# A trunk layer on one core: a bank of its own for the third product of a first pair, a norm stream that waits by GpSimd's price, and new prices for the planner

## The chip, the core and the metric

One core of one Trainium2 chip. The metric is the device time of the whole kernel in microseconds (us), the median of several runs. Engines are called by the profile's names: PE (TensorE), PEld (its weight loads), DVE (VectorE), ACT (ScalarE), POOL (GpSimd) and SP (SyncE, which issues the weight loads from memory).

## The reference

One layer of a streaming encoder, for 512 prompt tokens and 8x16 sample tokens (T = 640 in all), model width 1024, in fp32:

```python
z = x @ w_in
xa, ya, glu, q, gates = jnp.split(z, COL_SPLITS, axis=-1)
xa_c = causal_depthwise_conv(xa_hist, conv_a_w, conv_a_b)          # width 4
h, h_last = rg_lru(xa_c, h_prev, w_r, b_r, w_i, b_i, lam)          # gated linear scan
out_a = (h * jax.nn.gelu(ya)) @ proj_a
u = glu[..., :D_CONV] * jax.nn.sigmoid(glu[..., D_CONV:])
v = causal_depthwise_conv(u_hist, conv_b_w, conv_b_b)              # width 31
out_b = jax.nn.silu(layer_norm(v, ln_b_g, ln_b_b)) @ proj_b
out_c = mem_cross_attention(q, mem_k, mem_v) @ proj_c              # 4 heads, 256 memory tokens
merged = g[:, :, 0] * out_a + g[:, :, 1] * out_b + g[:, :, 2] * out_c
x = layer_norm(ALPHA * x + merged @ w_out, ln1_g, ln1_b)
ffn = (silu(x @ w_ffn_gate) * (x @ w_ffn_up)) @ w_ffn_down
x = layer_norm(ALPHA * x + ffn, ln2_g, ln2_b)
```

Prompt and sample tokens have different histories, states and memories: the prompt's memory is projected from mem_prompt, the sample's eight memories come from the caches cache_mem_k and cache_mem_v. The outputs are x, the new states and the prompt's memory.

## The kernel before

**Products.** Activations lie transposed, channels on the partitions and the 640 tokens along a row, in two halves of HT = 320 columns. Each fp32 product is made of three fp32r matmuls: the weight and the activation are each split in a high part (a rounded copy, written by ACT) and a low part (a subtract, on DVE, for some early weights on POOL, L305), and PE adds hi·hi, hi·lo and lo·hi in one PSUM bank. In the views `wh`/`wl` are the parts of a weight, `xh`/`xl` those of the layer's input, `s` is any tile of the common pool of row buffers, `pu` is a PSUM bank of the main loop (four buffers) and `pv` one of the side work (two buffers, counted in `side`).

**The main loop** runs over 304 steps, each with prep_hi (ACT), prep_lo, mm (PE) and an evacuation that is put off until the next flush. The order of the steps: mem_k and mem_v projections 0 to 7, the GLU and the query to 19, xa 20 to 27, the gates of branch C 28 to 35, proj_c 36 to 43 (from 304.3 us), the gates of branch B alternating with proj_b 44 to 59, ya 60 to 67, the gates of branch A 68 to 95, proj_a 96 to 103 (from 542.8 us), w_out to 116 (to 672 us), then the FFN, whose pairs begin with step 120 (686 us).

**Pairs.** The gates of branch A and the FFN's first two products take two 128-column blocks of weights at once and spend seven products in place of eight (`seven`): sums of weight blocks (on DVE) times sums of activation quarters (the streams sums0 and sums1, on DVE with a split by ACT and DVE). The first pair of each group uses the order m1, m4, m2, m6, m5, m7, m3. m1 goes to bank x; ACT copies it to `tmp["a"]`; the third product, m2, is then added in the same bank x, which so holds m1 + m2, one quarter of the result. m2's matmuls must therefore wait for the copy.

**Streams.** All other work is written as generators ("streams") that a planner interleaves with the main loop: attn (the cross-attention of prompt and sample), b (the width-31 conv and then ln_b_stream, its norm), lru (conv a, the gates r and i, the scan), a (times gelu, split in high and low for proj_a), the sums, the norms. The planner runs when the program is written, not on the chip, and it goes by prices: every instruction issued through `Engine` adds its price to that engine's time. After pieces of a step's matmuls `advance()` takes items of a stream as long as DVE's and ACT's priced times lie behind PE's:

```python
while max(V.time, 0 if name in vector_next else A.time) < P.time:
    c = next(gen)
    ...
    if c is None:
        break
```

A `yield None` in a stream thus means: no more of this stream in this call. `room()` holds a stream until a side bank is free, `over()` gives one back. `finish(name)` issues at once all that is left of a stream, ahead of the step that needs it: `finish("attn")` before proj_c (step 36), `finish("b")` before the first proj_b step (46), `finish("lru", "a")` before proj_a (96), the first sums before the pairs (the rows of the sums with the steps 68 and 120).

**The norm of branch B** (ln_b_stream). `total` adds the four rows of channels on POOL (L853 once, L855 twice); PE multiplies the sum with a matrix of ones to have it on all partitions; DVE subtracts, ACT squares; a second total; a second matmul; rs = pow on POOL (L892); then multiply, Silu and split, which gives bT for proj_b.

**The sample attention** (attn_sample). The keys and values of the caches are loaded by POOL's queue, one head of eight memories as four loads (L1069). After scores and softmax come the transposes of the probabilities, then for each head h 16 small matmuls (32 rows of output each) with the values of head h, which give back that head's four buffers. The tail copies the output, transposes it four times and splits it to cT for proj_c.

POOL itself isn't priced before the change; its queue runs in the order in which the planner issued it.

Of the kernel before, what the change touches and what calls it, by code (L numbers as in the profile page):

```python
# [11 lines left out]
OP = mybir.AluOpType  # L12
# [8 lines left out]
HT = T // 2  # L21
# [46 lines left out]
def elements(x):  # L68
    n = 1
    for d in x.shape[1:]:  # L70
        n *= d
    return n


def price_vector(e, name, a, k):
    if name in ("tensor_reduce", "bn_stats"):
        return 70 + elements(a[1]) / 0.96
    n = elements(a[0])
    if name == "tensor_tensor_scan":
        return 70 + 2 * n / 0.96  # L80
    if name in ("tensor_scalar", "tensor_copy", "memset"):
        return 70 + n / 1.92
    return (130 if name == "scalar_tensor_tensor" else 70) + n / 0.96


TABLES = {AF.Exp: "e", AF.Tanh: "esgl", AF.Sigmoid: "s", AF.Sqrt: "q", AF.Silu: "l", AF.Gelu_apprx_tanh: "g"}
# [2 lines left out]
def price_scalar(e, name, a, k):  # L89
    if name != "activation":  # L90
        return 100
    t = 130 + elements(a[0]) / 1.2
    t += 93 * sum(1 for z in ("scale", "bias", "accum_out") if z in k and not isinstance(k[z], float))
    need = TABLES.get(a[2])
    if need is not None and (e.table is None or e.table not in need):
        e.table = need[0]
        t += 1283
    return t


def price_tensor(e, name, a, k):
    n = elements(a[0])
    if a[1].dtype == F32R:
        return n / 2.4 + 2.5
    if a[0].shape[0] == 32:
        return n / 2.4
    return max(105.0, (n if name == "transpose" else 4 * n) / 2.4)
# [36 lines left out]
def trunk(ctx, tc, x_prompt, x_sample, mem_prompt, state_conv_a, state_lru, state_conv_b, cache_mem_k, cache_mem_v,  # L144
# [4 lines left out]
          new_conv_a_s, new_lru_s, new_conv_b_s):  # L149
    nc = tc.nc  # L150
    V, A, P = Engine(nc.vector, price_vector), Engine(nc.scalar, price_scalar), Engine(nc.tensor, price_tensor)
    G, S = nc.gpsimd, nc.sync

    w_in, proj_a, proj_b, proj_c, w_out = w_in[0], proj_a[0], proj_b[0], proj_c[0], w_out[0]
    w_mem_k, w_mem_v = w_mem_k[0], w_mem_v[0]
# [23 lines left out]
    def pv():  # L179
        assert side[0] < 2  # L180
        side[0] += 1
        return ps.tile([128, 2, 512], F32, name="pv", tag="v", bufs=2)

    def room(n=1):
        while side[0] + n > 2:
            yield None

    def over(n=1):
        side[0] -= n
# [134 lines left out]

    def advance(few=False):

        for e in (V, A):
            e.time = max(e.time, state["since"])
        state["since"] = P.time
        for item in list(streams):  # L330
            name, gen = item
            if few and name not in often:
                continue
            while max(V.time, 0 if name in vector_next else A.time) < P.time:
                try:
                    c = next(gen)
                except StopIteration:
                    streams.remove(item)
                    done.add(name)
                    break  # L340
                vector_next.discard(name)
                if c is None:
                    break
                if c == "v":
                    vector_next.add(name)

    def until(cond):

# [501 lines left out]
    def ln_b_stream():  # L850
        def total(x):
            y = get([128, T])
            G.tensor_tensor(y, x[0], x[1], op=OP.add)  # L853
            for k in range(2, KC):
                G.tensor_tensor(y, y, x[k], op=OP.add)  # L855
            return y

        y = total(vb)
        yield 1
        yield None  # L860
        yield from room()
        p = pv()
        P.matmul(p[:, 0], ones, y[:, :512], start=True, stop=True)
        P.matmul(p[:, 1, :128], ones, y[:, 512:], start=True, stop=True)
        free(y)
        yield None
        over()
        sq = []
        for k in range(KC):
            V.tensor_sub(vb[k][:, :512], vb[k][:, :512], p[:, 0])  # L870
            V.tensor_sub(vb[k][:, 512:], vb[k][:, 512:], p[:, 1, :128])
            x = get([128, T])
            A.activation(x, vb[k], AF.Square)
            sq.append(x)
            yield 1
        y = total(sq)
        free(*sq)
        yield 1
        yield None
        yield None  # L880
        yield from room()
        p = pv()

        for t in range(5):
            P.matmul(p[:, 0, t * 100:(t + 1) * 100], y[:, t * 128:(t + 1) * 128], ones[:, :100], start=True, stop=True)
        free(y)
        yield None
        over()
        ve = small.tile([128, 5], F32, name="ve5")
        V.tensor_scalar(ve, p[:, 0, :500].rearrange("p (t n) -> p t n", n=100)[:, :, 0], EPS, None, op0=OP.add)  # L890
        rs = small.tile([128, 5], F32, name="rs5")
        G.tensor_tensor(rs, ve, mhalf[:, :5], op=OP.pow)  # L892
        yield 1
        yield from room()
        p = token_row(rs)
        yield None
        over()
        for k in range(KC):
            V.tensor_mul(vb[k][:, :512], vb[k][:, :512], p[:, 0])
            V.tensor_mul(vb[k][:, 512:], vb[k][:, 512:], p[:, 1, :128])  # L900
            yield 1
        for k in range(KC):
            A.activation(vb[k], vb[k], AF.Silu, scale=pb[:, k, 32:33], bias=pb[:, k, 33:34])
# [603 lines left out]
    def seven(pair, put, following, first=False):  # L1507

        acc, tmp, late = {}, {}, []

        def fourth(p):
            put(0, 1, p, tmp["b"][:, 0], OP.subtract)

        def fifth(p):
            put(1, 1, p, tmp["b"][:, 0], OP.add)
            if first:
                V.tensor_tensor(tmp["a"][:, 1], tmp["a"][:, 1], p, op=OP.add)

        def after(n, p):
            if n == "m1":  # L1520
                tmp["a"], tmp["b"] = get([128, 2, HT]), get([128, 2, HT])
                copy(tmp["a"][:, 0], p)
            elif n == "m6":
                V.tensor_tensor(tmp["a"][:, 1], tmp["a"][:, 0], p, op=OP.add)
            elif n == "m2":
                put(0, 0, p, None, None)
            elif n == "m7":
                V.tensor_tensor(tmp["b"][:, 0], tmp["a"][:, 0], p, op=OP.add)
                for f in late:
                    f()  # L1530
            elif n in ("m4", "m5"):
                f = lambda: (fourth if n == "m4" else fifth)(p)
                if first:
                    late.append(f)
                else:
                    f()
            else:
                free(tmp["b"])
                put(1, 0, p, tmp["a"][:, 1], OP.add)
                free(tmp["a"])  # L1540

        products = PRODUCTS
        if first:

            products = [PRODUCTS[i] for i in (0, 5, 2, 1, 4, 3)] + [("m3", "x", True, "s4", "22")]
        for i, (n, u, opens, xn, wn) in enumerate(products):
            def mm(w, u=u, opens=opens, xn=xn):
                if opens:
                    acc[u] = pu(1)[0][:, :HT]
                p = acc[u]  # L1550
                hi, lo = w
                xhi, xlo = quarters[xn]
                for k in range(half):
                    P.matmul(p, hi[:, k], xhi[k], start=opens and k == 0, stop=False, skip_group_check=not opens)
# [404 lines left out]
```

## Time and profile before

| | us |
|---|---|
| median of 3 runs | 1100.15 |
| the runs | 1099.13, 1100.15, 1100.48 |
| the profiled run | 1099.67 |
| its span in the profile | 1097.9 |
| PE busy | 1061.7 (97%) |
| DVE busy | 802.9 (73%) |
| ACT busy | 490.1 (45%) |
| POOL busy | 165.3 (15%) |
| granted TensorE clock, mean | 0.99 |

The span runs from the first to the last instruction of the profile; the run's own time is 1.8 us longer. In the timeline a row has its start, its length, engine, line, operation and tiles; a number in brackets is the engine's idle time just before it, with what ended it. Nearly every instruction is issued in the helper at L64, so that a line says little: the tile names tell which step it is. POOL's instructions before the change are not issued through that helper and so keep their lines.

### The profile page before, as it was taken

How to read it: one execution, taken by the hardware profiler on the slowest of the kernel's cores; microseconds unless marked ns; L12 is line 12 of the kernel's file. 1: busy time of each engine (PE TensorE's matmuls, PEld its weight loads, DVE VectorE, ACT ScalarE, POOL GpSimd, SP SyncE). 2: the span in 40 equal slices, each digit the busy share in tenths (PEclk: the TensorE clock that was granted, in tenths of full speed). 3: DMA queues.
4: the chain of work that ended last, by engine and by line, in shares of the span. 5: the costliest groups of instructions: out<-in, count | busy, mean ns of one | idle time of the engine just before them, and what ended most of it. 6: DMA issues, size and time to landing. Idle time of an engine off the chain costs nothing.

```text
span 1097.9 us, 17000 instructions
## 1 busy us (share of the span) xinstructions
PE 1061.7 (97%) x6827; PEld 1005.9 (92%) x6827; DVE 802.9 (73%) x1335; ACT 490.1 (45%) x863; POOL 165.3 (15%) x185
## 2 busy tenths in 40 slices
PE   8799898998999999999999999899999999999997
PEld 6699898997999999999999889899999999888886
DVE  6929898996364873779855678888887887544775
ACT  4532645446648445846523124433444444334341
POOL 3623323556200000010001120000000000100111
PEclk9999999998999999999999999999999999999999
DMA  9732123352412121212325331132222322734481
GB/s 340 253 95 78 39 67 97 118 154 65 147 52 83 59 96 59 95 45 78 115 78 172 135 134 59 39 101 92 77 78 85 108 77 78 287 115 137 162 289 45
DMA packets 80334, 123.11 MB, mean 112 GB/s; under 512 B 4075, under 2 KB 59371, under 8 KB 80256
## 3 DMA queue, kind: packets, MB, share of 16 engines
q1 hardware_dynamic: 73168, 100.36, 27.6%
q0 software_dynamic: 7088, 21.68, 6.2%
q8 instruction: 53, 0.87, 0.3%
q14 instruction: 25, 0.20, 0.1%
HBM read 112.41 MB, written 9.61 MB: 111 GB/s over the span
## 4 chain that ended last, share of the span: by engine, by line
PE 70%; DVE 11%; ACT 4%; issue 1%; DVEq 0%; ACTq 0%
PE pu L64 62%; DVE s L64 10%; PE pv L64 8%; ACT s L64 3%; ACT L64 1%; DVE wl L64 1%; ACT wh L64 0%; DVE xres L64 0%; DVE mx L64 0%; DVE wh L64 0%; DVE xl L64 0%; DVE nm L64 0%; DVEq L1955 0%; ACT wl L64 0%; DVE st L64 0%
## 5 line engine op out<-in xcount | busy, mean ns | idle before, releaser
L64 PE MATMUL pu<-xh,wh 128*128 128x320 f32 x1040 | 252.6, 315 | 8.3 <-ACT s L64 7.1
L64 PE MATMUL pu<-xh,wl 128*128 128x320 f32 x1040 | 246.9, 310 | 0.0
L64 ACT ACTIVATE wh<-wr 128x1024 fp32r<-128x1024 f32 (+1 forms) x149 | 134.9, 908 | 229.1 <-PE pu L64 123.2
L64 PE MATMUL pu<-xl,wh 128*128 128x320 f32 x888 | 219.7, 311 | 0.0
L64 PEld LDWEIGHTS pu<-xh,wh 128*128 128x128 f32 x1040 | 178.1, 190 | 13.2 <-ACT s L64 9.1
L64 PE MATMUL pu<-s,wh 128*128 128x320 f32 x1064 | 185.5, 310 | 1.9 <-DVE s L64 1.3
L64 PEld LDWEIGHTS pu<-xh,wl 128*128 128x128 f32 x1040 | 177.4, 189 | 0.1
L64 DVE TENSOR_TENSOR s<-s,s 128x640 fp32r<-128x640 f32 (+4 forms) x176 | 124.5, 723 | 65.5 <-ACT s L64 63.3
L64 PEld LDWEIGHTS pu<-s,wh 128*128 128x128 f32 x1064 | 163.4, 188 | 3.4 <-DVE s L64 2.4
L64 DVE TENSOR_TENSOR wl<-wr,wh 128x1024 fp32r<-128x1024 f32 (+1 forms) x100 | 114.1, 1141 | 66.7 <-ACT wh L64 66.7
L64 PEld LDWEIGHTS pu<-xl,wh 128*128 128x128 f32 x888 | 154.2, 189 | 0.6 <-DVE xl L64 0.6
L64 DVE TENSOR_TENSOR s<-s,pu 128x320 f32<-128x320 f32 x188 | 88.4, 484 | 85.8 <-PE pu L64 83.3
L64 PE MATMUL pu<-s,wl 128*128 128x320 f32 x808 | 147.3, 310 | 0.9 <-DVE s L64 0.9
L64 DVE SCALAR_TENSOR_TENSOR s<-s,pb,s 128x511 f32<-128x511 f32 (+14 forms) x240 | 130.1, 613 | 7.8 <-ACT s L64 7.8
L64 ACT ACTIVATE s<-s 128x640 fp32r<-128x640 f32 (+4 forms) x144 | 87.9, 629 | 101.9 <-DVE s L64 101.8
L64 PEld LDWEIGHTS pu<-s,wl 128*128 128x128 f32 x808 | 126.1, 188 | 1.1 <-issue 1.1
L64 PE MATMUL pu<-wh,s 128*128 128x512 f32 (+1 forms) x396 | 116.2, 386 | 0.3 <-ACT wh L64 0.3
L64 PEld LDWEIGHTS pu<-wh,s 128*128 128x128 f32 x396 | 73.1, 189 | 15.1 <-ACT wh L64 1.2
L64 ACT ACTIVATE s<-pu 128x320 f32<-128x320 f32 (+2 forms) x90 | 36.7, 442 | 68.1 <-PE pu L64 68.0
L64 PE MATMUL pu<-wl,s 128*128 128x512 f32 (+1 forms) x198 | 62.9, 389 | 1.6 <-POOL wl L305 0.8
L305 POOL TENSOR_TENSOR wl<-wr,wh 128x1024 fp32r<-128x1024 f32 x13 | 44.4, 3418 | 81.2 <-ACT wh L64 68.4
L64 PE MATMUL pv<-wh,s 128*128 128x512 f32 (+1 forms) x152 | 48.7, 367 | 0.4 <-DVE xres L64 0.4
(139 smaller groups left out, 1249.0 us busy)
## 6 DMA issues: line engine op xcount, KB each, us to landing
wr<-in_w_in SPq DMA_DIRECT2D x26, 1024.0 KB, 5.1
wr<-in_w_ffn_down SPq DMA_DIRECT2D x19, 1024.0 KB, 5.1
wr<-in_w_ffn_gate SPq DMA_DIRECT2D x11, 1024.0 KB, 5.3
wr<-in_w_ffn_up SPq DMA_DIRECT2D x11, 1024.0 KB, 5.3
s<-in_cache_mem_k POOLq DMA_DIRECT2D x16, 256.0 KB, 7.0
s<-in_cache_mem_v POOLq DMA_DIRECT2D x16, 256.0 KB, 7.2
wr<-in_proj_a SPq DMA_DIRECT2D x4, 1024.0 KB
wr<-in_w_out SPq DMA_DIRECT2D x4, 1024.0 KB, 5.7
```

The source lines that it names most:

```text
L64: return f(*a, **k)
L305: self.eng.tensor_tensor(l, x, f32(h), op=OP.subtract)
```

## The change

1. **Prices.** The planner's prices for DVE, ACT and PE rise, and POOL is priced for the first time. For DVE the fixed part goes from 70 to 146 ns (tensor_reduce and bn_stats to 110, scalar_tensor_tensor from 130 to 230), for ACT from 130 to 180, for PE's fp32r matmuls from 2.5 to 13.3. POOL goes through `Engine` too, and `advance` keeps its time along with the others'.
2. **settle.** In ln_b_stream the fixed numbers of `yield None` become `settle(G)`: the stream gives nothing more until PE's priced time has passed POOL's. `total` first lifts POOL's time to that of DVE and ACT.
3. **The third product of a first pair** gets a PSUM bank of its own from the side banks (`u == "v"`), so it need not wait for the copy of m1; its evacuation adds `tmp["a"]` and the bank on DVE and then applies the function, in place of the function on bank x alone. That is one DVE tensor_tensor of 128x320 more per first pair, two in all.

```diff
 def price_vector(e, name, a, k):
...
-    return (130 if name == "scalar_tensor_tensor" else 70) + n / 0.96
+    return (230 if name == "scalar_tensor_tensor" else 146) + n / 0.951
+
+
+def price_pool(e, name, a, k):
+    if name == "dma_start":
+        return 600
+    return 150 + 3.2 * elements(a[0])
...
-    G, S = nc.gpsimd, nc.sync
+    G, S = Engine(nc.gpsimd, price_pool), nc.sync
...
     def advance(few=False):
 
-        for e in (V, A):
+        for e in (V, A, G):
             e.time = max(e.time, state["since"])
...
+    def settle(*engines):
+
+        t = max(e.time for e in engines or (V, A))
+        yield None
+        while P.time < t:
+            yield None
...
         def total(x):
             y = get([128, T])
+            G.time = max(G.time, V.time, A.time)
...
         y = total(vb)
         yield 1
-        yield None
+        yield from settle(G)
         yield from room()
...
         y = total(sq)
         free(*sq)
         yield 1
-        yield None
-        yield None
+        yield from settle(G)
...
         G.tensor_tensor(rs, ve, mhalf[:, :5], op=OP.pow)
         yield 1
+        yield from settle(G)
         yield from room()
...
             elif n == "m2":
-                put(0, 0, p, None, None)
+                if first:
+                    put(0, 0, p, tmp["a"][:, 0], OP.add)
+                    over()
+                else:
+                    put(0, 0, p, None, None)
...
             products = [PRODUCTS[i] for i in (0, 5, 2, 1, 4, 3)] + [("m3", "x", True, "s4", "22")]
+            products[2] = ("m2", "v", True, "12", "21")
...
             def mm(w, u=u, opens=opens, xn=xn):
-                if opens:
+                if u == "v":
+                    until(lambda: side[0] < 2)
+                    acc[u] = pv()[:, 0, :HT]
+                elif opens:
                     acc[u] = pu(1)[0][:, :HT]
```

The numbers of instructions stay nearly the same: two more DVE adds (the new puts), and 30 ACT table loads where there were 25, because the planner now mixes the streams' functions in another order. What moves is the order.

On POOL, around the norm's totals (L853 and L855: three adds of 128x640) and the loads of values for the sample's heads 2 and 3 (four loads each), before:

```order
L853 TENSOR_TENSOR s_184_2877<-s_170_2805,s_171_2809 128x640
L855 TENSOR_TENSOR s_184_2877<-s_184_2877,s_182_2871 128x640
L855 TENSOR_TENSOR s_184_2877<-s_184_2877,s_183_2875 128x640
L305 TENSOR_TENSOR wl<-wr,wh 128x1024
L1069 DMA s_188_2971<-in_cache_mem_v 128x4x128
L1069 DMA s_189_2972<-in_cache_mem_v 128x4x128
L1069 DMA s_190_2973<-in_cache_mem_v 128x4x128
L1069 DMA s_191_2974<-in_cache_mem_v 128x4x128
L1069 DMA s_196_3033<-in_cache_mem_v 128x4x128
L1069 DMA s_197_3034<-in_cache_mem_v 128x4x128
L1069 DMA s_198_3035<-in_cache_mem_v 128x4x128
L1069 DMA s_199_3036<-in_cache_mem_v 128x4x128
```

Both totals are issued before these eight loads (the adds shown are the second total; the first stands 13 rows further up). After:

```order
L64 DMA s_187_3068<-in_cache_mem_v 128x4x128
L64 DMA s_188_3069<-in_cache_mem_v 128x4x128
L64 DMA s_189_3070<-in_cache_mem_v 128x4x128
L64 DMA s_190_3071<-in_cache_mem_v 128x4x128
L64 TENSOR_TENSOR s_191_3076<-s_61_870,s_77_1346 128x640
L64 TENSOR_TENSOR s_191_3076<-s_191_3076,s_117_2040 128x640
L64 TENSOR_TENSOR s_191_3076<-s_191_3076,s_141_2465 128x640
L64 DMA s_195_3131<-in_cache_mem_v 128x4x128
L64 DMA s_196_3132<-in_cache_mem_v 128x4x128
L64 DMA s_197_3133<-in_cache_mem_v 128x4x128
L64 DMA s_198_3134<-in_cache_mem_v 128x4x128
```

The first total has moved behind head 2's loads and stands ahead of head 3's; the second comes after all of them.

On PE, the end of step 35 and the start of proj_c (the ones matmul of the norm, `pv<-...,ones`, stood in the middle of step 30 before, among the gates' matmuls), after:

```order
L64 MATMUL pv<-s_197_3133,s_185_2993 32x128
L64 MATMUL pv<-s_198_3134,s_185_2993 32x128
L64 MATMUL pv<-s_191_3076,ones 128x512
L64 MATMUL pv<-s_191_3076,ones 128x128
L64 MATMUL pv<-ident,s_206_3267 128x128 x4
L64 MATMUL pu<-s_97_1827,wh 128x320 x2
L64 MATMUL pu<-s_98_1828,wh 128x320 x2
L64 MATMUL pu<-s_97_1827,wl 128x320 x2
```

Head 3's matmuls, the ones matmul, the attention's last transposes and proj_c's first matmuls (with the splits s_97 and s_98 of those transposes) now follow each other without any matmul of a main step between.

On DVE, before proj_a (step 96): `s<-...,pu` are evacuations of the last pair, `wl<-wr,wh` weight subtracts, the 128x640 rows the a stream's multiplies and subtracts. Before:

```order
L64 TENSOR_TENSOR s_346_5716<-s_263_4533,s_345_5715 128x640
L64 TENSOR_TENSOR s_347_5739<-s_341_5658,pu 128x320
L64 TENSOR_TENSOR wl<-wr,wh 128x1024
L64 TENSOR_TENSOR s_344_5696<-s_341_5658,pu 128x320
L64 TENSOR_TENSOR wl<-wr,wh 128x1024
L64 TENSOR_TENSOR s_347_5739<-s_340_5657,pu 128x320
L64 TENSOR_TENSOR wl<-wr,wh 128x1024
```

The first of these rows is the a stream's last. After:

```order
L64 TENSOR_TENSOR s_335_5695<-s_332_5615,pu 128x320
L64 TENSOR_TENSOR s_218_3540<-s_218_3540,s_289_4910 128x640
L64 TENSOR_TENSOR s_339_5751<-s_218_3540,s_338_5750 128x640
L64 TENSOR_TENSOR s_252_4439<-s_252_4439,s_295_4982 128x640
L64 TENSOR_TENSOR s_341_5756<-s_252_4439,s_340_5755 128x640
L64 TENSOR_TENSOR s_258_4531<-s_258_4531,s_303_5058 128x640
L64 TENSOR_TENSOR s_343_5761<-s_258_4531,s_342_5760 128x640
L64 TENSOR_TENSOR s_262_4651<-s_262_4651,s_306_5122 128x640
L64 TENSOR_TENSOR s_345_5766<-s_262_4651,s_344_5765 128x640
L64 TENSOR_TENSOR s_267_4722<-s_267_4722,s_307_5156 128x640
L64 TENSOR_TENSOR s_347_5771<-s_267_4722,s_346_5770 128x640
L64 TENSOR_TENSOR wl<-wr,wh 128x1024
```

Five blocks of the a stream (a multiply and a subtract each, with a copy on ACT between) stand behind the last evacuation of the pairs, issued by `finish("lru", "a")`.

More of the change, by code (lines that the diff above doesn't have):

```diff
@@ L76, in price_vector @@
     if name in ("tensor_reduce", "bn_stats"):
-        return 70 + elements(a[1]) / 0.96
+        return 110 + elements(a[1]) / 0.96
     n = elements(a[0])
     if name == "tensor_tensor_scan":
-        return 70 + 2 * n / 0.96
+        return 146 + 2 * n / 0.951
     if name in ("tensor_scalar", "tensor_copy", "memset"):
         return 70 + n / 1.92
-    return (130 if name == "scalar_tensor_tensor" else 70) + n / 0.96
+    return (230 if name == "scalar_tensor_tensor" else 146) + n / 0.951
[3 more added lines that the diff above has]
+    return 150 + 3.2 * elements(a[0])
 TABLES = {AF.Exp: "e", AF.Tanh: "esgl", AF.Sigmoid: "s", AF.Sqrt: "q", AF.Silu: "l", AF.Gelu_apprx_tanh: "g"}
@@ L91, in price_scalar @@
         return 100
-    t = 130 + elements(a[0]) / 1.2
+    t = 180 + elements(a[0]) / 1.164
     t += 93 * sum(1 for z in ("scale", "bias", "accum_out") if z in k and not isinstance(k[z], float))
@@ L103, in price_tensor @@
     if a[1].dtype == F32R:
-        return n / 2.4 + 2.5
+        return n / 2.4 + 13.3
     if a[0].shape[0] == 32:
```

## The prediction

> **What bounds the kernel now.** I read the page's busy shares and its chain first, then PE's waits, then the timeline at each wait, then windows around them.
>
> ```profile
> PE 1061.7 (97%) x6827; PEld 1005.9 (92%) x6827; DVE 802.9 (73%) x1335; ACT 490.1 (45%) x863; POOL 165.3 (15%) x185
> PE 70%; DVE 11%; ACT 4%; issue 1%; DVEq 0%; ACTq 0%
> ```
>
> PE is busy for 1061.7 of 1097.9 us: 36.2 us of idle is all that an order of work can win, apart from clock. DVE has 27% of room in the mean, which says nothing of a stage. Who ends PE's waits:
>
> ```profile
> PE pu L64 <- ACT s L64: 7.6, 4, 4.3
> PE pv L64 <- POOL s L855: 5.0, 1, 5.0
> PE pv L64 <- DVE s L64: 3.6, 5, 1.6
> PE pu L64 <- DVE s L64: 3.1, 4, 1.0
> ```
>
> Columns: total us, times, longest. Where they stand (the bracket is idle time and releaser):
>
> ```profile
> 107.56 0.81 PE L64 MATMUL pu<-xh,wh 128*128 128x320 f32 x2 [0.98 <-DVE s L64]
> 116.78 1.01 PE L64 MATMUL pv<-s,s 128*128 128x256 f32 x6 [0.67 <-DVE s L64]
> 118.14 0.86 PE L64 MATMUL pv<-s,s 128*128 128x256 f32 x5 [0.34 <-DVE s L64]
> 136.82 0.74 PE L64 MATMUL pu<-xh,wh 128*128 128x320 f32 x2 [2.30 <-ACT s L64]
> 168.90 1.09 PE L64 MATMUL pv<-ident,s 128*128 128x128 f32 x8 [1.15 <-ACT s L64]
> 187.57 2.66 PE L64 MATMUL pv<-s,s 128*128 128x256 f32 x20 [1.62 <-DVE s L64]
> 253.17 2.07 PE L64 MATMUL pv<-s,ones 128*128 128x512 f32 x2 [5.00 <-POOL s L855]
> 694.12 0.51 PE L64 MATMUL pu<-xh,wh 128*128 128x320 f32 x1 [4.32 <-ACT s L64]
> ```
>
> Six waits lie at 107 to 188 us (7.06 us together), one is the norm's at 253, one the first FFN pair's at 694. The long ones also cost clock; the windows (busy us of PE, PEld, DVE, ACT, POOL, then granted clock):
>
> ```profile
> 120.00:140.00 20.00, 17.70 (x116) 17.29 (x115) 16.75 (x33) 14.25 (x32) 10.58 (x24) 0.95 0.17 54
> 140.00:160.00 20.00, 20.00 (x139) 19.70 (x137) 18.15 (x37) 9.76 (x26) 2.77 (x2) 0.97 0.16 53
> 180.00:200.00 20.00, 18.38 (x130) 18.14 (x129) 20.00 (x39) 7.68 (x27) 8.96 (x11) 1.00 0.40 118
> 240.00:260.00 20.00, 15.01 (x93) 12.93 (x92) 15.99 (x28) 8.86 (x19) 11.26 (x13) 0.83 0.42 129
> 686.00:698.00 12.00, 7.68 (x42) 7.42 (x42) 11.65 (x18) 3.75 (x8) 0.00 (x0) 0.86 0.00 0
> ```
>
> After the 2.30 us wait the clock misses 5% and 3% of 20 us, 1.6 us. After the 1.62 us wait it misses nothing. At 253 it misses 17% of 20 us, 3.4 us, of which I put half into the wait itself: 1.7.
>
> **The front's waits (gain 8.2).** The higher prices send the same stream items to DVE and ACT later relative to PE's matmuls, so at steps 8 to 27 their queues hold less ahead of what PE waits for. By 187 DVE is busy 20.00 of 20 us: the wait there is queue. I take all six waits and the 1.6 us of clock, 8.7, less 0.5 left at 136. Lower bound: only the three DVE waits up to 118 go, 2.0. Upper: 8.7.
>
> **The norm's stream (gain 6.7).** The first ones matmul moves from step 30 to the end of step 35, behind three POOL adds that are long done: 5.00 plus 1.7 of clock; less than 5.0 only if the adds themselves come late. settle puts no wait on an engine: it holds back the stream's own next item until PE's priced time has passed, and behind it wait only that stream's items. Proj_b, which needs them, is due at step 46, and the order has them all by 45. So settle costs nothing by itself; if the stream were not done by 45, proj_b would wait as proj_a does below.
>
> **First pairs (gain 0.7).** The third product gets a bank of its own, for which no other stream has to be pushed on, and its hi half (8 matmuls) no longer waits for ACT's copy of the first product. In the first FFN pair that copy is late because ACT and DVE drain forced sums, and the lo half needs a DVE subtract behind the same sums:
>
> ```profile
> 693.65 0.42 ACT L64 ACTIVATE s<-pu 128x320 f32<-128x320 f32 x1
> 694.00 0.68 DVE L64 TENSOR_TENSOR wh<-wr,wh 128x512 fp32r<-128x512 f32 x1
> ```
>
> DVE is busy 11.65 of 12 us there: it is what is late next, and the change adds one more sums split ahead and one put (0.48) behind. So the 4.32 us doesn't go; the hi matmuls move into the idle time, worth 0.3 (from -0.5 to 1.6, if the clock returns too); 0.4 for the w_in pair.
>
> **New wait 1: head 3 of the sample attention (cost 4.4).** On POOL the norm's three adds now stand between head 2's loads and head 3's.
>
> ```profile
> L1069 POOL DMA_DIRECT2D s<-in_cache_mem_v x16 | 11.9, 752 | 2.7 <-PE pv L64 2.7
> L855 POOL TENSOR_TENSOR s<-s,s 128x640 f32<-128x640 f32 x4 | 6.7, 1674 | 11.1 <-DVE s L64 8.1 <-ACT s L64 2.9
> L853 POOL TENSOR_TENSOR s<-s,s 128x640 f32<-128x640 f32 x2 | 3.6, 1780 | 2.2 <-ACT s L64 2.2
> s<-in_cache_mem_v POOLq DMA_DIRECT2D x16, 256.0 KB, 7.2
> 543.35 0.46 PE L64 MATMUL pu<-s,wl 128*128 128x320 f32 x2
> 544.23 0.46 PE L64 MATMUL pu<-s,wl 128*128 128x320 f32 x2
> ```
>
> Head 0's matmuls free the buffers for head 2's last load and for the adds. From there POOL needs 0.75 + (1.78 + 2x1.67) + 3x0.75 + 7.2 = 15.3 us to the last landing. A step of 6 matmuls takes 0.88 us (544.23 - 543.35), 0.147 each; PE has 84 of them, 12.4, and 0.1 of small ones ahead of head 3. Wait 2.8 (1.5 to 4.5), and, as after 2.30, 1.6 of clock.
>
> **New wait 2: proj_c's start (cost 1.7).** The attention stream is forced at step 36 with its tail unissued; the copies to the split run behind a Square that waits for the norm's subtract.
>
> ```profile
> 256.56 1.66 DVE L64 TENSOR_TENSOR s<-s,pv 128x512 f32<-128x512 f32 x4
> 260.18 1.35 ACT L64 ACTIVATE s<-s 128x640 f32<-128x640 f32 x2
> 297.77 0.76 ACT L64 ACTIVATE s<-pv 128x128 fp32r<-128x128 f32 x4
> 293.31 0.60 PE L64 MATMUL pv<-ident,s 128*128 128x128 f32 x4
> ```
>
> After the ones matmul: half of 1.66, half of 1.35, a quarter of 0.76, three handovers at 0.1, together 2.0, against some 0.4 us of transposes on PE: 1.7 (1 to 2.3). Before, nothing was left to force here.
>
> **New wait 3: proj_a's start (cost 5.9).** Before, the a stream ended ahead of proj_a; now five of its eight blocks are forced at step 96. Each is mul on DVE, copy on ACT, sub on DVE, and DVE's row has mul, sub, mul, sub.
>
> ```profile
> 529.89 0.82 DVE L64 TENSOR_TENSOR s<-s,s 128x640 f32<-128x640 f32 x1
> 530.80 0.74 ACT L64 ACTIVATE s<-s 128x640 fp32r<-128x640 f32 x1 [0.31 <-DVE s L64]
> 531.66 0.82 DVE L64 TENSOR_TENSOR s<-s,s 128x640 fp32r<-128x640 f32 x1
> 538.70 0.82 DVE L64 TENSOR_TENSOR s<-s,s 128x640 fp32r<-128x640 f32 x1
> 542.77 0.75 PE L64 MATMUL pu<-s,wh 128*128 128x320 f32 x4
> ```
>
> A block takes 1.77 us from mul to sub and some 0.75 more before the next mul: 2.52. Step 96 starts at 542.8, DVE is free 0.6 later, the first forced lo is there at 0.6 + 1.77 + 0.82 = 3.2, the fifth at 13.3; PE then has 4 matmuls, so it ends at 13.9. Unhindered it has 8 transposes (0.87) and 48 matmuls (7.06), 7.9. Cost 5.9 (4 to 7.5, the latter with a dip of clock).
>
> **Small things.** ACT has five more table loads; I price them at nothing, since ACT is busy 45%.
>
> ```profile
> L64 ACT ACT_TABLE_LOAD x25 | 32.1, 1283 | 14.4 <-DVE nm L64 9.4 <-issue 2.9 <-PE pu L64 1.1
> 289.55 1.28 ACT L64 ACT_TABLE_LOAD   x1
> 290.84 3.36 ACT L64 ACTIVATE s<-s,pb 128x640 f32<-128x640 f32 x4
> ```
>
> Uncovered they would cost 5x1.28 = 6.4. The Trainium skill (ScalarE: Activation LUTs, What ACT_TABLE_LOAD costs) adds a drain to each, 2.66 us a switch; by that 13.3 us uncovered, and a forecast 6.9 higher at the worst. The trace disagrees: the activation starts 1.29 us after the load. ACT's other short waits (7.6 - 4.32 - 2.30 = 1.0) reappear at other steps: 0.5 more.
>
> **Sum.** -8.2 - 6.7 - 0.7 + 4.4 + 1.7 + 5.9 + 0.5 = -3.1. The profiled run took 1099.67 us (span 1097.9 and 1.8 around it), 0.5 under the median of 1100.15. So 1096.6 for such a run, **1097.1** as a median. A measurement here can tell 0.2%, 2.2 us, from no change.
>
> **The rivals.**
> - *The front's waits stay* (slower). They could be serial chains within a stream, moved with it, not queues. For it: ACT had 5.75 us free at 120 to 140, and still PE waited 2.30. Against: DVE was full at 187. Then -6.7 - 0.7 + 12.5 = +5.1: 1105.3. It decides once less than 2.9 of the 8.2 go. Chance 0.17.
> - *POOL is stretched* (slower). POOL's weight subtract shows how unequal one shape can be (min/median/max ns):
>
> ```profile
> L305 POOL TENSOR_TENSOR wl<-wr,wh x13: 2373/2842/6735, 38.1 to 281.4; 128x1024 fp32r<-128x1024 f32 x13
> ```
>
>   The three adds now run while DVE does the conv's taps. At 6735/2842 they take 12.2 instead of 5.1, all of it in head 3's wait: +4.0, 1104.2. It decides from 5.3 us of stretch. The Trainium skill (SBUF — State Buffer, SBUF: two separate sides) says that a DVE operation with two SBUF inputs and a GpSimd operation that reads SBUF exclude each other for a whole instruction. Against: the adds' own rows differ by little (1.67 and 1.78 mean). Chance 0.06.
> - *The new waits 1 and 2 are covered* (faster): the loads land earlier than by the median, or PE comes later. Then only proj_a's is left: -15.6 + 5.9 + 0.5 = -9.2, 1091. Chance 0.14.
> - *The change only shifts waits*: the same idle at other places, 1100. Chance 0.07.
> - My forecast: 0.56. Its own range, from the bounds of the terms, is 1091 to 1103; I give 0.34 of it to faster by over 0.2%, 0.17 to within, 0.05 to slower.
>
> **The chances.** Faster 0.34 + 0.14 = 0.48; same 0.17 + 0.07 + 0.03 (of the first rival) = 0.27; slower 0.05 + 0.14 + 0.06 = 0.25. To hold 8 in 10 the range goes from 1089, inside the covered case, to 1105.5, over both slower rivals' centres.
>
> **What would show it.** Right: no wait of PE on L855's successor at the norm's ones matmul; no waits over 1 us between 100 and 200; a wait of about 3 us for head 3's loads and 1.7 at proj_c's first matmuls near 300 us; at proj_a's first step five waits of some 1.6 us each on DVE; at the first FFN pair still 3 to 4 us idle, now ended by DVE. Wrong: waits over 2 us in the front, or proj_a starting dense.

## The result and the profile after

The changed kernel takes 1105.74 us (median of 6 runs, 1104.08 to 1108.51) against 1099.92 for the kernel before, measured beside it: a ratio of 1.0055, with a 95% interval of 1.0042 to 1.0068. It is 0.55% slower. The forecast was 1097.1, a little faster, with a range of 1089 to 1105.5.

The profiled execution after took 1108.51 us (span 1106.7, mean clock 0.984), so 2.8 us over the median; before it was 1099.67 (0.99). The page's busy shares and its chain:

```profile
PE 1070.4 (97%) x6827; PEld 1012.8 (92%) x6827; DVE 800.2 (72%) x1337; ACT 498.2 (45%) x868; POOL 181.7 (16%) x185
PE 82%; ACT 6%; DVE 5%; POOL 3%; DMA 2%; issue 2%; SPq 0%; DVEq 0%; POOLq 0%; ACTq 0%
```

PE's idle time is 36.3 us where it was 36.2, and its busy time 8.7 us longer with the same matmuls: the waits have moved, not shrunk, and more matmuls run at a low clock. Who ends the waits now (total, times, longest):

```profile
PE pu L64 <- ACT s L64: 10.4, 11, 2.7
PE pu L64 <- DVE s L64: 4.9, 8, 2.0
PE pv L64 <- DVE wh L64: 4.5, 1, 4.5
```

The norm's line of POOL is gone; ACT has 11 waits where it had 4. Where they stand:

```profile
132.34 0.74 PE L64 MATMUL pu<-xh,wh 128*128 128x320 f32 x2 [0.59 <-ACT s L64]
252.32 1.05 PE L64 MATMUL pu<-xh,wh 128*128 128x320 f32 x2 [2.73 <-ACT s L64]
294.14 0.56 PE L64 MATMUL pu<-s,wh 128*128 128x320 f32 x2 [1.40 <-ACT s L64]
499.97 0.39 PE L64 MATMUL pu<-xh,wl 128*128 128x320 f32 x1 [1.98 <-DVE s L64]
544.33 0.56 PE L64 MATMUL pu<-s,wh 128*128 128x320 f32 x2 [1.24 <-ACT s L64]
546.69 0.56 PE L64 MATMUL pu<-s,wh 128*128 128x320 f32 x2 [0.65 <-ACT s L64]
702.91 1.43 PE L64 MATMUL pv<-xh,wh 128*128 128x320 f32 x4 [4.50 <-DVE wh L64]
```

Of the six waits at 107 to 188 us one of 0.59 is left. But there is a wait of 2.73 at 252 us, one at proj_c's start, one of 1.98 in the pairs, the forced tail at proj_a from 544 us, and the FFN's, as long as ever. The windows around them (busy us of PE, PEld, DVE, ACT, POOL, then the granted clock):

```profile
120.00:140.00 20.00, 19.41 (x138) 18.99 (x137) 17.97 (x35) 11.79 (x30) 8.09 (x22) 1.00 0.30 97
240.00:260.00 20.00, 17.27 (x107) 16.11 (x106) 14.49 (x27) 12.87 (x24) 5.34 (x5) 0.83 0.49 146
280.00:300.00 20.00, 18.34 (x158) 16.59 (x158) 10.63 (x21) 9.53 (x18) 7.42 (x7) 0.91 0.18 54
540.00:560.00 20.00, 15.55 (x72) 12.66 (x70) 12.62 (x17) 7.84 (x11) 4.11 (x8) 0.83 0.22 65
700.00:720.00 20.00, 17.09 (x97) 17.09 (x98) 16.88 (x30) 10.07 (x20) 0.00 (x0) 0.83 0.17 53
```

The clock is back at 120 to 140 us, still 0.83 at 240 to 260, and newly low at 280 to 300 and at 540 to 560, where it was 1.00 before. The start of main steps in both timelines shows where the time went (side work lies at other places between them, so the middle rows say less than the last ones):

| step | before | after | after - before |
|---|---|---|---|
| 16, GLU | 107.56 | 106.70 | -0.9 |
| 32, gates | 267.99 | 252.32 | -15.7 |
| 36, proj_c | 304.31 | 292.35 | -12.0 |
| 68, pairs | 491.10 | 484.67 | -6.4 |
| 96, proj_a | 542.77 | 540.20 | -2.6 |
| 98, proj_a's third step | 556.85 | 564.26 | +7.4 |
| 125, FFN pairs | 701.04 | 709.88 | +8.8 |

The first two steps of proj_a lose 10.0 us. Between step 68 and step 96 3.8 us are lost; 0.9 of them are eight transposes (`pv<-ident,hout`) that ran ahead of step 68 before and run just ahead of step 96 now, so the pairs of branch A lose 2.9. From step 125 on nothing changes.

### The profile page after: what moved, and what is told of

It is laid out like the page before. It is cut to its first block, busy times and chain, and to the rows that moved or that the text cites. A ratio compares the mean times of both kernels' runs of the same rounds, so it can differ in the third digit from the quotient of the medians.

```text
span 1106.7 us, 16996 instructions
## 1 busy us (share of the span) xinstructions
PE 1070.4 (97%) x6827; PEld 1012.8 (92%) x6827; DVE 800.2 (72%) x1337; ACT 498.2 (45%) x868; POOL 181.7 (16%) x185
## 4 chain that ended last, share of the span: by engine, by line
PE 82%; ACT 6%; DVE 5%; POOL 3%; DMA 2%; issue 2%; SPq 0%; DVEq 0%; POOLq 0%; ACTq 0%
PE pu L64 71%; PE pv L64 11%; ACT s L64 4%; DVE s L64 3%; ACT L64 1%; POOL s L64 1%; POOL wl L64 1%; DVE wl L64 1%; DMA s<-in_cache_mem_k 1%; ACT wh L64 1%; DMA s<-in_w_mem_k 0%; DMA wr<-in_proj_a 0%; DVE xres L64 0%; DMA s<-in_x_prompt 0%; DVE wh L64 0%
## 5 line engine op out<-in xcount | busy, mean ns | idle before, releaser
L64 PE MATMUL pu<-xh,wh 128*128 128x320 f32 x1024 | 246.6, 313 | 5.3 <-ACT s L64 5.2
L64 PE MATMUL pu<-xl,wh 128*128 128x320 f32 x880 | 216.9, 310 | 0.0
L64 PE MATMUL pu<-s,wh 128*128 128x320 f32 x1064 | 192.1, 316 | 7.4 <-ACT s L64 5.0
L64 DVE TENSOR_TENSOR s<-s,s 128x640 fp32r<-128x640 f32 (+4 forms) x176 | 129.1, 748 | 89.4 <-ACT s L64 87.3
L64 PEld LDWEIGHTS pu<-xh,wh 128*128 128x128 f32 x1024 | 174.7, 189 | 9.7 <-ACT s L64 6.7
L64 PEld LDWEIGHTS pu<-s,wh 128*128 128x128 f32 x1064 | 167.1, 192 | 11.9 <-ACT s L64 7.2
L64 PE MATMUL pu<-s,wl 128*128 128x320 f32 x808 | 149.8, 314 | 0.6 <-DVE s L64 0.6
L64 PEld LDWEIGHTS pu<-s,wl 128*128 128x128 f32 x808 | 128.7, 192 | 0.8 <-issue 0.8
L64 DVE SCALAR_TENSOR_TENSOR s<-s,pb,s 128x511 f32<-128x511 f32 (+14 forms) x240 | 120.6, 573 | 5.2 <-ACT s L64 5.2
L64 POOL TENSOR_TENSOR wl<-wr,wh 128x1024 fp32r<-128x1024 f32 x13 | 61.1, 4700 | 107.5 <-ACT wh L64 94.2
```

The costliest lines, as they stand in the source:

```text
L64: return f(*a, **k)
```

## The experiments

All kernels compute the whole reference. Ratios are to the kernel before, on the same chip. They are not ratios of the medians shown, so a difference taken from the one can be some tenths of a us off the other:

| run | median us | ratio | 95% interval |
|---|---|---|---|
| the change | 1105.74 | 1.0055 | 1.0042 to 1.0068 |
| e1_bank | 1100.24 | 1.0001 | 0.9992 to 1.0010 |
| e2_settle | 1104.23 | 1.0036 | 1.0023 to 1.0048 |
| e4_no_bank | 1105.18 | 1.0047 | 1.0035 to 1.0060 |
| e5_ahead | 1100.11 | 1.0001 | 0.9993 to 1.0010 |
| e6_lru_sp | 1106.83 | 1.0061 | 1.0048 to 1.0074 |
| e7_lo_first | 1103.95 | 1.0031 | 1.0021 to 1.0040 |
| e8_attn_first | 1108.58 | 1.0078 | 1.0064 to 1.0092 |
| e9_ahead_late | 1103.30 | 1.0029 | 1.0018 to 1.0039 |
| e10_evac_first | 1098.82 | 0.9990 | 0.9982 to 0.9999 |
| e11_ramp | 1101.08 | 1.0010 | 1.0001 to 1.0019 |
| e12_three | 1092.36 | 0.9934 | 0.9920 to 0.9947 |
| e13_old_prices | 1098.48 | 0.9987 | 0.9978 to 0.9996 |

### The parts of the change, one at a time

**e1_bank**, the kernel before with part 3 alone:

```diff
+            products[2] = ("m2", "v", True, "12", "21")
...
-                if opens:
+                if u == "v":
+                    until(lambda: side[0] < 2)
+                    acc[u] = pv()[:, 0, :HT]
```

> The kernel before with the third product of a first pair in its own bank and nothing else. Theory A (DVE, full with the forced sums, is what the first FFN pair waits for; the bank only moves the hi matmuls into the idle time): the wait at the first FFN pair stays at 4 us or more and is ended by DVE; time within 1.5 us of the kernel before, about 1099.5. Rival (the copy by ACT was the bound, and another part of the change spoils the gain): the 4.3 us wait and its clock go, 1094 to 1095.

The timeline of PE at the first FFN pair:

```profile
694.86 0.86 PE L64 MATMUL pv<-xh,wh 128*128 128x320 f32 x4 [3.77 <-DVE wh L64]
```

No change in time, and the wait is ended by DVE's weight subtract: theory A, though the wait is 3.77 us and not 4 or more. The bank alone buys nothing.

**e2_settle**, the kernel before with part 2 and the price of POOL that it needs, at the old prices of DVE, ACT and PE:

```diff
-        yield None
+        yield from settle(G)
```

> The kernel before with POOL priced and the norm's stream held by settle, at the old prices of DVE, ACT and PE, without the bank. Theory A (the loss at proj_a and in the later pairs is due to the raised prices, which send the streams later): no wait over 1 us at proj_a; the norm's 5.0 us wait goes, the waits from 107 to 188 us stay as before, some of the gain returns as a wait on ACT near the softmax: 1094 to 1098. Rival (holding the norm back is what pushes the lru and a streams behind, so that they are forced at proj_a): waits of 4 us or more in sum at proj_a, 1102 or more.

Neither theory. Proj_a starts densely and the six early waits stay, as theory A has it, but the kernel is 4 us slower. PE's timeline where the norm's 5.00 us wait stood, and in the first pair of branch A's gates (the w_in pair):

```profile
257.79 1.05 PE L64 MATMUL pu<-xh,wh 128*128 128x320 f32 x2 [6.65 <-ACT s L64]
498.13 0.51 PE L64 MATMUL pu<-xh,wh 128*128 128x320 f32 x1 [3.94 <-ACT s L64]
```

The wait on POOL is gone, and one of 6.65 us on ACT, at the start of the next step (31), has taken its place. A second new wait stands where the later streams meet the forced sums. So settle alone, without the raised prices, loses 0.36%, and the norm's wait was not alone. The forced tail at proj_a is not there: it comes only with the raised prices.

**e4_no_bank**, the change without part 3 (the diff above, left out).

> The changed kernel without the third product's own bank: prices and settle alone. Theory A (the bank is worth nothing either way): within 1.5 us of the changed kernel, 1104 to 1107; the first FFN pair's wait is back on ACT at about 4.3 us. Rival (the extra put on DVE and the side bank cost time in the pairs): 1101 to 1103.

```profile
698.74 0.64 PE L64 MATMUL pu<-xh,wh 128*128 128x320 f32 x1 [5.05 <-ACT s L64]
```

As theory A: within 1 us of the change, with the FFN's wait back on ACT's copy (5.05 us, foretold at about 4.3). Prices and settle together make the whole loss. Against e2_settle this run adds the raised prices of DVE, ACT and PE alone: the six early waits go (one of 0.64 is left), the forced tail comes, and the time changes by 0.11 points of ratio, which the intervals don't tell from nothing. The raised prices without settle were not run.

### The wait at 252 us

What ACT and DVE do ahead of it in the changed kernel:

```profile
245.72 1.21 DVE L64 TENSOR_REDUCE mx<-pv 128x4 f32<-128x1024 f32 x1
247.20 1.28 ACT L64 ACT_TABLE_LOAD   x1 [2.14 <-issue]
250.44 1.28 ACT L64 ACT_TABLE_LOAD   x1
251.74 0.94 ACT L64 ACTIVATE s<-pu,pa 128x320 f32<-128x320 f32 x2
```

DVE's maximum of the sample softmax ends at 246.9; ACT, which waits for it from 245.1 on, loads a table, makes four exponentials, loads the next table and only then evacuates the two banks that PE needs. DVE itself stood idle ahead of that maximum, for ACT's copies of the lru's gate weights:

```profile
243.45 2.35 DVE L64 TENSOR_TENSOR s<-s,s 128x512 fp32r<-128x512 f32 x2 [6.49 <-ACT s L64]
```

**e6_lru_sp**: ACT's and DVE's work just ahead waits for the lru's gate weights, which POOL loads.

```diff
-            G.dma_start(raw, w[0, 4 * q:4 * q + 4].rearrange("n c d -> c n d"))
+            S.dma_start(raw, w[0, 4 * q:4 * q + 4].rearrange("n c d -> c n d"))
```

> The changed kernel with the loads of the lru's gate weights on SP's queue in place of POOL's. Theory B (at 252 us PE waits 2.7 us for ACT because ACT's copies and DVE's subtracts of those weights stand in order ahead of the softmax and wait for loads that POOL issued late, behind a weight subtract of 11.4 us): the wait at 252 us shrinks below 1 us, with its clock 2 to 5 us less than the changed kernel, 1100 to 1103. Rival (the softmax's own chain of DVE maximum, two table loads and four exponentials is what is long): the wait stays at 2.5 to 3 us, time within 1.5 us of the changed kernel.

```profile
242.89 0.63 ACT L64 ACTIVATE s<-s 128x512 fp32r<-128x512 f32 x1 [0.45 <-DMA s<-in_lru_w_r]
252.60 0.83 PE L64 MATMUL pu<-xh,wh 128*128 128x320 f32 x2 [2.73 <-ACT s L64]
```

The wait is the same 2.73 us, as the rival has it, but the run does not decide against theory B. SP issued the first load at 233.65 us, behind a load of w_in's weights, 2.4 us earlier than POOL in the change (236.08), and ACT still could not copy it before 242.89 (242.78 in the change): the weights came no earlier, so the chain that theory B names was left as it was. Why they came no earlier was not tried.

**e10_evac_first**: the evacuation goes to ACT ahead of the softmax.

```diff
         free(*qs)
+        flush()
         pr = softmax_start(acc)
```

> The changed kernel with the pending evacuation of the gates issued on ACT ahead of the sample softmax. Theory C (PE's 2.7 us wait at 252 us is only ACT's order: the evacuation stands behind four exponentials and two table loads, which wait for DVE's maximum): no wait over 0.7 us between 245 and 260 us, the granted clock of 240 to 260 us goes from 0.83 back to 0.95 or more; 3 to 5 us less than the changed kernel, 1101 to 1103. Rival (DVE's or the loads' lateness reaches PE by another way, as the weight subtract behind the same queue): a wait of 1.5 us or more remains before 275 us, time within 1.5 us of the changed kernel.

The windows at 240 and at 280 us:

```profile
240.00:260.00 20.00, 20.00 (x148) 19.19 (x147) 17.21 (x32) 15.97 (x29) 10.31 (x10) 1.00 0.44 134
280.00:300.00 20.00, 18.83 (x148) 17.65 (x142) 11.14 (x26) 9.15 (x18) 4.68 (x3) 1.00 0.17 53
```

PE is dense through the window and the clock is whole: theory C. The gate weights are as late here as in the change, so the order on ACT alone is enough to remove the wait. The kernel gains 0.65 points of ratio on the change, some 7 us, more than the 3 to 5 expected: the clock at proj_c (280 to 300 us) comes back with it, though a wait of 0.9 us stays there.

### The start of proj_c

**e8_attn_first**: the norm's ones matmul waits for the end of the attention.

```diff
         yield from settle(G)
+        while "attn" not in done:
+            yield None
```

> The changed kernel with the norm's first ones matmul held until the attention stream is through, so that proj_c's copies no longer stand behind the norm's subtract and square. Theory A (that chain is the 1.7 us wait at 294 us, and the half clock after it costs as much again): the wait at proj_c falls below 0.8 us, the granted clock of 280 to 300 us returns to 1.0; 1.5 to 4 us less than the changed kernel. Rival (the norm comes later and is forced at the first proj_b, or the wait is the output's copy and not the square): the same idle at proj_c or new waits at step 46, time within 1.5 us of the changed kernel.

```profile
292.11 0.56 PE L64 MATMUL pu<-s,wh 128*128 128x320 f32 x2 [0.47 <-ACT s L64]
347.06 1.76 PE L64 MATMUL pu<-s,wh 128*128 128x320 f32 x4 [4.92 <-ACT s L64]
```

Theory A is right on the place: proj_c's wait falls from 1.40 to 0.47, and the clock of 280 to 300 us is 1.00. But the rival has the cause: the norm is now forced at the first proj_b, 4.92 us, and the kernel is 2.8 us slower than the change, more than the rival's 1.5.

### The forced tail at proj_a

**e5_ahead**: lru and a may run 4 us of priced time ahead of PE in the pairs.

```diff
+            ahead = 4000 if name in ("lru", "a") and state["i"] >= first["pairs"] else 0
-            while max(V.time, 0 if name in vector_next else A.time) < P.time:
+            while max(V.time, 0 if name in vector_next else A.time) < P.time + ahead:
```

> The changed kernel, but from the pairs on the lru and a streams may run 4 us of priced time ahead of PE, so that four of the five blocks of the a stream that were forced at proj_a are issued before it. Theory A (the forced tail costs 4.4 us of waits and some 4 us of half clock in one step, and DVE and ACT have room for it in the pairs): proj_a starts without a wait over 0.5 us, 7 to 10 us less than the changed kernel, 1096 to 1099. Rival (DVE has no room in the pairs, so the same work makes waits there): waits of 1 us and more at steps 76 to 95, 1102 to 1106.

The window of proj_a's start, and what stands at the first pair:

```profile
540.00:560.00 20.00, 20.00 (x138) 20.00 (x137) 12.52 (x17) 7.63 (x10) 0.00 (x0) 1.00 0.46 155
480.00:500.00 20.00, 15.02 (x82) 14.09 (x81) 14.88 (x28) 10.69 (x23) 0.00 (x0) 0.83 0.01 1
489.49 0.85 PE L64 MATMUL pv<-xh,wh 128*128 128x320 f32 x4 [1.85 <-DVE wh L64]
```

Proj_a is dense at full clock, and the kernel is level with the one before: 5.6 us less than the change. The forced tail is a cause. The gain is less than the 7 to 10 us foretold: some is lost again at the first pair, where DVE now runs three of the lru's scans (1.49 us each, from 487.4 us on) ahead of the pair's weight subtracts.

**e9_ahead_late** (6 us, from the thirteenth step of the pairs) and **e11_ramp** (0.5 us more at each step from the ninth on, up to 8) spread the same work otherwise:

```diff
+            ahead = 6000 if name in ("lru", "a") and state["i"] >= first["pairs"] + 12 else 0
```

```diff
+            ahead = min(8000, max(0, 500 * (state["i"] - first["pairs"] - 8))) if name in ("lru", "a") and "pairs" in first else 0
```

> As the run that let the lru and a streams run ahead of PE, but only from the middle of the second pair on and by 6 us. Theory A (running ahead cost 5 us of waits at the first pair, where the forced sums fill DVE, and nothing later): the waits at 489 to 500 us are those of the changed kernel again, 2.9 us of loss in that window and not 8.2, proj_a starts without a wait over 0.5 us; 7 to 10 us less than the changed kernel, 1096 to 1099. Rival (the streams' work makes waits of its own in whichever pairs it is put): 1100 to 1103.

> The changed kernel with the lru and a streams let ahead of PE by 0.5 us more at each step of the pairs, up to 8 us, from the ninth step on. Theory A (the streams' work fits in the pairs if it is spread; the 4.0 us wait of the last try came from letting 6 us of it in at once): no wait over 1.2 us between 505 and 560 us; 6 to 9 us less than the changed kernel, 1097 to 1100. Rival (DVE is too full in the pairs however the work is spread): waits of 2 us and more in sum between 505 and 540 us, 1101 to 1104.

One wait of each:

```profile
514.69 3.54 PE L64 MATMUL pu<-s,wl 128*128 128x320 f32 x12 [3.97 <-DVE s L64]
```

```profile
533.74 0.41 PE L64 MATMUL pu<-xh,wl 128*128 128x320 f32 x1 [2.02 <-ACT s L64]
```

Neither reaches the 6 to 10 us: 2.4 and 4.7. At once, the work makes one wait of 3.97; spread, waits of 0.91 and 2.02. The rival is nearer, and for e11_ramp it holds: the pairs have room in the mean, but in the three ways tried the work put there is partly waited for.

### The first FFN pair

**e7_lo_first**: the third product's weight subtract goes ahead of the forced sums.

```diff
+        while new and s.early:
+            new.pop(0).prep_lo()
         if s.before:
             s.before()
```

> The changed kernel with the third product's weight subtract on DVE put ahead of the forced sums of a first pair. Theory A (with the bank of its own that subtract is all that holds the third product's lo half; after it PE waits for the fourth product's sums): the third product runs through, the 4.5 us wait at 703 us falls to 2 to 3.5 us and moves to the fourth product; 1 to 3 us less than the changed kernel, 1102.5 to 1104.5. Rival (the sums are ready no earlier than before, so the wait only moves by as much): total wait at that pair within 0.5 us of 4.5, no change, 1104.5 to 1106.5.

```profile
700.02 3.48 PE L64 MATMUL pu<-s,wl 128*128 128x320 f32 x12 [2.97 <-ACT wl L64]
```

As theory A: the third product runs through, the wait falls to 2.97 us and is the fourth's. 1.8 us less than the change.

**e13_old_prices** puts that subtract and the bank in the kernel before (the diffs of e1_bank and e7_lo_first).

> The kernel before with the third product's own bank and its subtract ahead of the forced sums, at the old prices and without settle. Theory A (the bank is worth something only together with that subtract): the wait at the first FFN pair falls from 4.3 to about 3 us and no half clock follows the w_in pair; 1 to 3 us less than the kernel before, 1097 to 1099. Rival (the sums of the fourth product are the bound, so the wait moves there in full): within 1 us of the kernel before.

```profile
694.21 2.02 PE L64 MATMUL pu<-s,wl 128*128 128x320 f32 x12 [2.24 <-ACT wl L64]
```

1.5 us less than the kernel before: the bank and the early subtract together are worth something, where the bank alone was not. The subtract without the bank was not run. The wait is 2.24 and not 3, with 0.88 and 0.64 at the next two products.

### The three together

**e12_three** has the diffs of e7_lo_first, e10_evac_first and e11_ramp.

> The changed kernel with the three repairs together: the evacuation ahead of the softmax, the third product's subtract ahead of the forced sums, the streams let ahead step by step. Theory (the three losses are apart in time and add): 11 to 15 us less than the changed kernel, 1091 to 1095, below the kernel before by 0.5% or more. Rival (what is won in one place is waited for in the next): 1096 to 1100.

1092.36 us, 0.66% below the kernel before and 13.4 us below the change: the repairs add, within the noise (about 7, 4.7 and 1.8). It beats both kernels.

## Why the prediction was wrong

**The front's waits (-8.2): right.** Step 16 is 0.9 us earlier; of the six waits one of 0.59 remains, and the clock of 120 to 140 us is 1.00. With the old prices (e2_settle) all six stay; with the new ones they go without the bank too (e4_no_bank). In rows, 7.06 - 0.59 = 6.5 of waits and 1.6 of clock.

**The norm's stream (-6.7): wrong, the costliest miss.** I wrote "less than 5.0 only if the adds themselves come late", and "settle costs nothing by itself". The adds were in time, but a second wait stood in the shadow of the first. The backlog of conv taps on DVE that made the norm's sum late makes the softmax's maximum late too; ACT waits for that in order, with an evacuation behind. POOL's last add in the kernel before, then DVE and ACT in e2_settle:

```profile
251.58 1.53 POOL L855 TENSOR_TENSOR s<-s,s 128x640 f32<-128x640 f32 x1 [8.12 <-DVE s L64]
236.99 13.92 DVE L64 SCALAR_TENSOR_TENSOR s<-s,pb,s 128x491 f32<-128x491 f32 x20
250.83 1.21 DVE L64 TENSOR_REDUCE mx<-pv 128x4 f32<-128x1024 f32 x1
252.67 1.28 ACT L64 ACT_TABLE_LOAD   x1 [8.91 <-DVE nm L64]
```

Before, PE stood still at 253 us anyway, and ACT caught up. e2_settle shows it bare: 5.00 on POOL becomes 6.65 on ACT, and settle alone costs 4 us. With the new prices it is 2.73 and a clock of 0.83; there the taps are through, and the maximum stands behind the lru's late gate weights instead. e10_evac_first shows that the order on ACT is what turns a late maximum into a wait of PE. I had followed every queue up to the wait that goes, and not asked what PE would meet next if it came there 5 us earlier.

**First pairs (-0.7): the mechanism right, the size not.** What ACT and DVE do at the FFN's:

```profile
701.83 0.42 ACT L64 ACTIVATE s<-pu 128x320 f32<-128x320 f32 x1
702.17 0.69 DVE L64 TENSOR_TENSOR wh<-wr,wh 128x512 fp32r<-128x512 f32 x1
```

The hi matmuls moved into the idle time, DVE's subtract ends the wait, and 4.50 us stay, as foretold; from step 98 to step 125 1.4 us are lost, not 0.3 won: the clock after the wait is low for longer (0.83 at 700 to 720 us). At the w_in pair a wait of 1.98 on DVE came that I did not have: lru work (a scan of 1.49 us that ends at 499.4), issued later than before, stands ahead of an evacuation there. Branch A's pairs lose 2.9 us in all.

**New wait 1, head 3 (+4.4): wrong, there is none.**

```profile
276.09 5.67 POOL L64 TENSOR_TENSOR s<-s,s 128x640 f32<-128x640 f32 x3
281.71 2.99 POOL L64 DMA_DIRECT2D s<-in_cache_mem_v  x4
s<-in_cache_mem_v POOLq DMA_DIRECT2D x16, 256.0 KB, 5.2
285.07 1.08 PE L64 MATMUL pv<-s,s 128*32 128x128 f32 x32
289.80 1.08 PE L64 MATMUL pv<-s,s 128*32 128x128 f32 x32
```

The queue is as I saw it, and the adds took 5.67 (forecast 5.1). But a load lands in 5.2 us at the median, not 7.2, and these four took 3.8 to 4.1: the last, issued at 283.95, is there at 288.1, ahead of head 3 at 289.80. And I had counted "0.1 of small ones" for the matmuls of two heads on the way, which take 1.08 us per head: a row that was in the trace of before.

**New wait 2, proj_c (+1.7): right in its waits**, 1.40 and 0.27. Without a price for it came a clock of 0.91 at 280 to 300 us, 1.8 us.

**New wait 3, proj_a (+5.9): right in kind, too small.** In the trace steps 96 and 97 take 24.06 us (540.20 to 564.26) where they took 14.08: 10.0 are lost. (The eight transposes that I had put in this step ran ahead of it.) ACT, ahead of the first block and at a later one, and DVE:

```profile
541.18 1.06 ACT L64 ACTIVATE wh<-wr 128x1024 fp32r<-128x1024 f32 x1 [2.25 <-DMA wr<-in_proj_a]
545.90 0.74 ACT L64 ACTIVATE s<-s 128x640 fp32r<-128x640 f32 x1 [1.62 <-DVE s L64]
546.67 1.56 DVE L64 TENSOR_TENSOR s<-s,s 128x640 fp32r<-128x640 f32 x2 [0.80 <-ACT s L64]
```

The period is 2.36 us (forecast 2.52), but the first copy waits on ACT until 543.55 for proj_a's weights and the lru's last outputs: the first low part is there 4.9 us after the step's start, not 3.2. And PE comes out of it at half clock, which costs 1.35 us in step 97 and more within 96. I had named that dip as the bound of the range, 7.5, and not taken it; 10.0 lies beyond even that.

**Small things.** One slip in the sum that no run bears on: a price of 13.3 for the five table loads in place of nothing makes a forecast 13.3 higher, not 6.9.

**The sum.** The profiled execution took 8.8 us more than the one before. By windows and steps: the front won 8 to 9, the norm about 2 in place of 6.7, the pairs lost 4.3 (2.9 and 1.4) in place of winning 0.7, proj_c lost 3.5 in place of 1.7, proj_a 10.0 in place of 5.9; head 3 lost nothing. Most of the rest is two new waits on ACT among ya's steps (0.97 at 447.55 us, 0.90 at 477.35). The term that failed first is the norm's; with its new wait removed (e10_evac_first) the change is within 0.1% of the kernel before. The measured 1105.74 lies only 0.2 us above the range, but that is chance: the upper bound stood on two rivals, the front's waits staying and POOL's adds stretched, and neither came. That the change "only shifts waits" had 0.07; PE's idle time did stay the same, but the clock did not.

## What to carry over

A wait that is removed brings its engine earlier to the next wait: before pricing the gain, look in the same trace at what the other queues finish during the wait, since that is what becomes late. Where a planner orders the work, a `finish` that meets unfinished work is a serial chain at the slowest place; count what is left to force before and after. And see whether an evacuation can go ahead of a chain on its engine that waits for another engine: here that was worth some 7 us.

## What the hardware showed

**Half clock.** The length of a wait alone does not foretell it. In the change waits of 2.73 and 4.50 us were followed by a low clock (0.83 at 240 to 260 and at 700 to 720 us), and so was the 2.97 in e7_lo_first (0.91), while the same 2.97 in e12_three, at 688 us, left the clock whole. The 2.73 us wait at 252 us is there in e6_lru_sp and e7_lo_first as well, with a clock of 1.00 and 0.91 at 240 to 260 us. The clock records of these traces show it falling to half, for 3.41, 6.83 or 10.24 us at a time (6.83 at 252 us in the change, 3.41 in e7_lo_first, none in e6_lru_sp). In e10_evac_first the clock of the forced tail at proj_a was 0.77 although no wait there was over 1.2 us. The window of the FFN's wait and after it in e7_lo_first and in e12_three, and e10_evac_first's tail:

```profile
700.00:720.00 20.00, 19.74 (x122) 19.50 (x123) 17.89 (x34) 10.05 (x20) 0.00 (x0) 0.91 0.22 64
```

```profile
680.00:700.00 20.00, 15.50 (x102) 14.75 (x101) 18.46 (x31) 8.29 (x17) 0.00 (x0) 1.00 0.17 52
```

```profile
540.00:560.00 20.00, 19.72 (x100) 17.85 (x101) 12.24 (x16) 5.16 (x7) 0.00 (x0) 0.77 0.17 53
```

The Trainium skill (TensorE: Matmul & The Clock Gate, Why this matters for your kernels) asks for no PE-idle gaps over about 3 us between bursts. Here a single gap of 2.73 us was followed by it, and so were four of 0.30 to 1.12 us, 2.37 us in all within 5 us (e10_evac_first, from 534.3 us on), so the measurement is the stricter one. The same kernel's executions differed with it: the change's six runs lie between 1104.08 us at a mean clock of 0.991 and 1108.51 at 0.984.

**POOL beside DVE.** Beside an unbroken run of conv taps on DVE, POOL's weight subtract took up to 11.4 us, against 2.4 at its shortest:

```profile
203.05 11.25 POOL L64 TENSOR_TENSOR wl<-wr,wh 128x1024 fp32r<-128x1024 f32 x1 [4.92 <-PE pv L64]
221.78 11.38 POOL L64 TENSOR_TENSOR wl<-wr,wh 128x1024 fp32r<-128x1024 f32 x1
L64 POOL TENSOR_TENSOR wl<-wr,wh x13: 2392/2962/11379, 38.5 to 263.4; 128x1024 fp32r<-128x1024 f32 x13
```

DVE ran taps for 10.97 us of the first and 10.81 of the second. Before, the longest was 6.7, with taps for all of it; DVE has no more taps at 200 to 235 us than before (63 and 65), but the subtract runs beside others of them. That the taps stretch it is read from these rows and was not tested. So POOL was stretched, at another place than my rival had it, whose adds took 5.67: it delays POOL's loads there, and the one wait of PE on them is 0.2 us. The planner's price for this instruction is 150 + 3.2x1024, about 3.4 us.
